# Splitting the last group's left operands where they are made, and keeping three attention tasks under way

## The chip, the cores and the metric

The kernel runs on one core of a Trainium2 chip. A core has five engines that run side by side and meet at semaphores: TensorE (PE, the matmuls), VectorE (DVE), ScalarE (ACT), GpSimd (POOL) and SyncE (SP, which here only starts DMAs). Each takes its instructions in order, so an instruction that waits holds up everything behind it on its engine. The metric is the device time of one launch in microseconds (us). Three runs of the kernel before gave 1162.16, 1162.51 and 1163.85 us: a median of 1162.51.

## The reference, cut to what matters

Two sequences of 512 tokens (b = 0 and 1), model width D = 1024, go through one layer.

```python
h = rms_norm(x, norm1_g) * (1 + sc1) + sh1          # sc, sh, g from silu(c) @ w_ada + b_ada
q_a, k_a, v_a, q_r, k_r, v_r, g_r = split(h @ w_in)
o_a = windowed_attention(q_a, k_a, v_a, sink)       # 8 heads, 2 key groups, |t-s| <= 128, ALiBi
o_r = bidirectional_retention(q_r, k_r, v_r, g_r)   # 4 heads, two decays, group norm, swish gate
x = x + g1 * (concat(o_a, o_r) @ w_out)
h = rms_norm(x, norm2_g) * (1 + sc2) + sh2
x = x + g2 * (square(relu(h @ w_mlp1)) @ w_mlp2)    # 1024 -> 4096 -> 1024
y = rms_norm(x, final_g)
```

## The kernel before, in words

**Precision.** Every large product is made of three: each float32 operand is split into a high part (a cast to a reduced float32, fp32r, on ACT) and a low part (operand minus high part, a subtraction on DVE), and PE adds high x high, high x low and low x high. `split_to` (L840 to L842) is that pair: an ACT cast (L841) and a DVE subtraction (L842).

**The front, up to about 400 us.** Projections of both sequences are a list of units on PE (`run_units`). Beside them a queue of *stages* runs: eight `attn_block`s a sequence (one of four query blocks for one of two key groups) and four `ret_head`s a sequence. Each is a generator; `tick_stage` keeps two of them under way and lets one take a step between two pieces of projection. A `yield 2` asks for a pause of two such pieces before the next step, so that ACT, DVE and POOL finish before PE needs the result. Two of these pauses stand ahead of transposes on PE: `ppt` (L417, attention's probabilities) and `pyb` (L490, retention's normalised output). `norm_x1` prepares sequence 1 (x tiles, `x_rstd`, `x_scale`, then eight transposed columns) and is begun by a hook behind unit 9. The stages take PSUM from five `aux` banks.

**MLP 1, from about 500 to 829 us.** Products of 2x2 blocks are made in seven instead of eight products (Winograd's form of Strassen's algorithm), named P1, P2, P6, P7, P5, P4, P3. A `FirstPair` n (0 to 15) makes two rows of 128 hidden columns; its seven products are 12 matmuls each. Between them `prep` splits the next pair's weights. At its end `store` (L960) combines the squared-ReLU results into the seven *left operands* of MLP 2, each 128x512 float32 (256 KB), and writes them to DRAM through SP's queue (L970): `spill[g][p, :, i, :]`, with g = n // 4 the group and i = n % 4 the place in it. The results lie in tiles `u` (the squared blocks) and `s` (their sums).

**MLP 2, from about 829 us to the end.** Four groups g of seven products of 48 matmuls. `load_u(g, p)` brings back a left operand in two halves h of 512 KB (tiles `ur`, L1275), two steps ahead; `prep(g, p)` (L1278 on) splits it (tiles `uc`, high and low) and the weight block (tiles `wc`), one step ahead. So each `prep` issues four ACT casts and four DVE subtractions of 128x1024. `gather` adds the banks into four accumulators on DVE. The first pair of steps of MLP 2 is prepared within pair 15.

**The last group** runs P1, P2, P6, P7, P4, P5, P3. Here the result is also gated, added to the residual rows `x2r` (`final_rows` loads them behind P2), normalised and stored: `gated_sums` (L1349, L1350) for accumulators that are complete but for one product, `gated_bank` (L1356, L1357) for a bank straight from PE, `squares` (L1362 on ACT, L1365 on POOL), `finish` (L1369 on POOL, L1373 on DVE, then the output DMA). Quadrant (0,0) is gated behind P6 and (0,1) behind P7, with the squares of (0,0).

**What sets the order.** A scheduler places the instructions on each engine from the written order and its own costs; DMAs wrapped in `in_order` keep the written one. Buffers: 32 tiles `r4` and 4 tiles `lx` of 512 KB, 8 tiles `f2` of 256 KB. POOL starts few DMAs: two decay tables, the sink and eight rows of gates (L155, L156, L158, L292).

Of the kernel before, what the change touches and what calls it, by code (L numbers as in the profile page):

```python
# [30 lines left out]
def trunk_kernel(ctx, tc, x0, x1, c0, c1, w_ada, b_ada, norm1_g, w_in, attn_sink, decay_f, decay_b,  # L31
# [352 lines left out]
    def attn_block(b, g, i, qs, k_, a, mix):  # L384
# [27 lines left out]
        for hh in range(4):  # L412
            if hh % 2 == 0:
                nc.scalar.activation(st[hh][:, :w], st[hh][:, :w], AF.Copy, scale=rden[:, hh:hh + 1])
            else:
                nc.vector.tensor_scalar(st[hh][:, :w], st[hh][:, :w], rden[:, hh:hh + 1], None, ALU.mult)
        yield 2  # L417
        pts = []
# [21 lines left out]
    def ret_head(b, h, q_, k_, v_, sg, mix):  # L440
# [46 lines left out]
        for t in range(NT):  # L487
            nc.vector.tensor_scalar(yn[:, t * P:(t + 1) * P], pn[:, t * P:(t + 1) * P], mv[:, t, 0:1],
                                    rs[:, t:t + 1], ALU.subtract, ALU.mult)
        yield 2  # L490
        pb = aux_bank(f"pyb_{nm}")
# [84 lines left out]
    def tick_stage(force=False):  # L576

        while stages and len(active) < 2:
            kind, start = stages.pop(0)
            active.append([start(), 0, kind])  # L580
        for a in active:
            if a[1] <= clock[0] or force:
                wait = next(a[0], "end")
                if wait == "end":
                    active.remove(a)
                else:
                    a[1] = clock[0] + wait
                return True
        return False
# [244 lines left out]
    hc = [[None, None] for _ in range(7)]  # L834
    spill = [tc.dram_tile((7, P, GP, 512), F32, name=f"spill{g}") for g in range(NPAIR // GP)]

# [27 lines left out]
    class FirstPair:  # L864
# [95 lines left out]
        def store(self):  # L960
            c11, c12, c21, c22 = self.c
            two = [self.four(f"s_{self.n}_{i}") for i in range(2)]
            s1, s2, s3, s4 = [two[i // 2][:, i % 2, :] for i in range(4)]
            nc.vector.tensor_tensor(s1, c12, c22, ALU.add)
            nc.vector.tensor_sub(s2, s1, c11)
            nc.vector.tensor_sub(s3, c11, c12)
            nc.vector.tensor_sub(s4, c21, s2)
            g, i = divmod(self.n, GP)
            for p, t in ((P1, c11), (P2, c21), (P4, c22), (P5, s1), (P6, s2), (P7, s3), (P3, s4)):
                nc.sync.dma_start(spill[g][p, :, i, :], t)  # L970

# [213 lines left out]
    def norm_x1():  # L1185
        xt = [load_x_tile(1, t) for t in range(NT)]
        for t in range(NT):
            x_scale(xt[t], x_rstd(1, t, xt[t]))
        yield
        yield  # L1190
        for kc in range(KC):
# [5 lines left out]
    for h in range(RH):  # L1197
        units += ret_units(hT[0], 0, h)
    run_units(units, 1.3, {9: lambda: extra.append(norm_x1())}, pace=0.5)
    units = attn_units(hT[1], 1) + ret_v_units(hT[1], 1)  # L1200
# [81 lines left out]
    def prep(g, p):  # L1282
        for h in range(2):
# [8 lines left out]
            src = {P1: b11, P2: b21, P6: b11, P7: b12, P5: t1.get((g, h)), P4: b21, P3: b22}[p]  # L1292
            left[g, p, h] = split_pairs(f"uc_{g}_{p}_{h}", raw_u.pop((g, p, h)))
            right[g, p, h] = split_pairs(f"wc_{g}_{p}_{h}", src)
# [43 lines left out]
    def final_rows(i):  # L1338
        for t in range(4):
            r0 = (t // 2) * S + i * 256 + (t % 2) * P  # L1340
            fin["x", i, t] = r4f(f"x2r_{i}_{t}")
            in_order(nc.sync.dma_start(fin["x", i, t], x2s[r0:r0 + P, :]))
# [71 lines left out]
    for s, (g, p) in enumerate(steps[:-2]):  # L1414
# [14 lines left out]
        if final:  # L1429
            if p == P2:  # L1430
                final_rows(1)
                final_rows(0)
            elif p == P6:
                gated_sums((1, 0))
                gated_sums((0, 0))
            elif p == P7:
                gated_sums((1, 1))
                gated_sums((0, 1))
                for t in range(4):
# [38 lines left out]
```

## Time and profile before

| | value |
|---|---|
| runs, median of three | 1162.51 us (1162.16 to 1163.85) |
| the profiled execution's own time | 1161.89 us |
| its span in the profile | 1160.1 us (1.8 us below its own time) |
| PE busy | 1109.4 us, 96% |
| DVE busy | 933.4 us, 80% |
| ACT busy | 494.0 us, 43% |
| POOL busy | 69.0 us, 6% |
| DMA traffic | 224.37 MB, mean 193 GB/s |

The profile is one execution. An engine's share is an average over stages with different limits, so the views that matter are the ones by stretch of time: windows that give every engine's busy time and the clock granted to PE, the order of instructions in time on one engine, and the list of who waited for whom. In a row of instructions `out<-in` are the names of the program's tiles; in a row of the order in time the two numbers ahead are the start and the time of that row, and a bracket at the end is idle time before it and what ended it. Where such a row stands for several instructions (x2), consecutive ones overlap a little, so starts tell more than durations.

### The profile page before, as it was taken

The numbers are of one execution on the slowest core, as the hardware profiler recorded it, in microseconds if no ns is written. First come the engines' busy times: TensorE is split into PE (matmuls) and PEld (weight loads), VectorE is DVE, ScalarE is ACT, GpSimd is POOL, SyncE is SP. The second block draws the span as 40 slices with busy tenths as digits, with TensorE's granted clock in tenths as the row PEclk, the third lists the DMA queues.
The fourth block names the chain that finished last, engine by engine and source line by source line (L and its number), as shares of the span: only waits on it lengthen the run. The fifth ranks groups of instructions, "written<-read, shape, count | busy, mean of one in ns | idle before, by whom it ended". The sixth has DMA issues, their size and how long they took to land.

```text
span 1160.1 us, 14470 instructions
## 1 busy us (share of the span) xinstructions
PE 1109.4 (96%) x5167; PEld 903.8 (78%) x5167; DVE 933.4 (80%) x1550; ACT 494.0 (43%) x846; POOL 69.0 (6%) x79
## 2 busy tenths in 40 slices
PE   5899999999999999999999999999999999999975
PEld 3578787777888788888788888888778888888854
DVE  5888988978888697689998778866696866968896
ACT  4456765435563234346333333332455333432341
POOL 3620001000000000000000000000000000000012
PEclk9999999999999999999999999999999999999988
DMA  9796677655455489941654455443866364464413
GB/s 289 238 283 211 214 230 272 218 193 190 155 167 199 156 303 333 343 148 46 214 204 155 164 165 189 155 163 103 287 230 237 106 195 137 144 200 139 184 37 145
DMA packets 124112, 224.37 MB, mean 193 GB/s; under 512 B 8500, under 2 KB 59780, under 8 KB 124040
## 3 DMA queue, kind: packets, MB, share of 16 engines
q1 hardware_dynamic: 111144, 217.14, 55.8%
q10 hardware_dynamic: 12544, 6.29, 1.9%
q8 instruction: 40, 0.66, 0.3%
q0 software_dynamic: 352, 0.03, 0.1%
q14 instruction: 32, 0.26, 0.1%
HBM read 152.36 MB, written 71.06 MB: 193 GB/s over the span
## 4 chain that ended last, share of the span: by engine, by line
PE 75%; DVE 11%; DMA 5%; issue 3%; ACT 3%; POOL 2%; SPq 0%; ACTq 0%; DVEq 0%; POOLq 0%
PE px_None L936 12%; PE x L1310 12%; PE py_None L936 9%; PE y L1310 9%; PE po L129 2%; PE po L130 2%; PE po L128 2%; DMA raw_ada_g<-in_w_ada_dram 2%; PE po L429 1%; PE ppt L422 1%; PE psc L396 1%; PE pj_rq L129 1%; PE pj_rq L128 1%; PE pj_rv L128 1%; PE pj_rv L130 1%
## 5 line engine op out<-in xcount | busy, mean ns | idle before, releaser
L841 ACT CAST uc_0h<-ur 128x1024 fp32r<-128x1024 f32 x28 | 29.4, 1050 | 67.9 <-PE x L1310 38.1
L1310 PE MATMUL x<-wc_0l,uc_0h 128*128 128x512 f32 x128 | 50.7, 396 | 5.4 <-DVE wc_0l L842 5.4
L1310 PE MATMUL x<-wc_0h,uc_0h 128*128 128x512 f32 x128 | 50.5, 396 | 3.9 <-DVE acc L1356 3.2
L128 PE MATMUL po<-wh_wo,ms 128*128 128x512 f32 x128 | 50.5, 397 | 1.9 <-ACT ms L761 1.9
L1310 PE MATMUL x<-wc_1h,uc_1h 128*128 128x512 f32 x128 | 50.3, 394 | 1.0 <-ACT wc_1h L841 1.0
L1310 PE MATMUL x<-wc_1l,uc_1h 128*128 128x512 f32 x128 | 50.2, 392 | 0.5 <-DVE wc_1l L842 0.5
L1310 PE MATMUL x<-wc_0h,uc_0l 128*128 128x512 f32 x128 | 50.3, 393 | 0.0
L1310 PE MATMUL x<-wc_1h,uc_1l 128*128 128x512 f32 x128 | 50.1, 391 | 0.0
L129 PE MATMUL po<-wl_wo,ms 128*128 128x512 f32 x128 | 49.8, 391 | 0.3 <-DVE wl_wo L103 0.3
L842 DVE TENSOR_TENSOR uc_0l<-ur,uc_0h 128x1024 fp32r<-128x1024 f32 x28 | 34.2, 1222 | 19.6 <-ACT uc_0h L841 15.9
L130 PE MATMUL po<-wh_wo,ms 128*128 128x512 f32 x128 | 49.6, 390 | 0.0
L255 DVE SCALAR_TENSOR_TENSOR adacc_c<-raw_ada_c,cact,adacc_c 128x512 f32<-128x512 f32 x56 | 39.8, 748 | 6.7 <-DMA raw_ada_c<-in_w_ada_dram 5.7
L841 ACT CAST wc_s4h<-raw_w 128x1024 fp32r<-128x1024 f32 x16 | 16.8, 1053 | 62.8 <-PE px_None L936 46.1
L406 ACT ACTIVATE st<-st,negm 128x256 f32<-128x256 f32 (+1 forms) x64 | 35.2, 556 | 18.8 <-DVE negm L401 18.8
L841 ACT CAST wc_0h<-w 128x1024 fp32r<-128x1024 f32 x24 | 25.2, 1049 | 42.4 <-DVE w L1289 16.3
L255 DVE SCALAR_TENSOR_TENSOR adacc_g<-raw_ada_g,cact,adacc_g 128x512 f32<-128x512 f32 x56 | 40.3, 747 | 2.1 <-DMA raw_ada_g<-in_w_ada_dram 1.8
L842 DVE TENSOR_TENSOR wc_0l<-w,wc_0h 128x1024 fp32r<-128x1024 f32 x24 | 29.3, 1221 | 13.5 <-ACT wc_0h L841 13.4
L936 PE MATMUL py_None<-hch,wc_a 128*128 128x512 f32 x120 | 39.7, 390 | 0.1
L936 PE MATMUL px_None<-hch,wc_a 128*128 128x512 f32 x120 | 39.6, 391 | 0.0
L936 PE MATMUL px_None<-hch,wc_s 128*128 128x512 f32 x120 | 39.4, 389 | 0.0
L1310 PE MATMUL y<-wc_1l,uc_1h 128*128 128x512 f32 x96 | 37.5, 391 | 0.6 <-DVE wc_1l L842 0.6
L1310 PE MATMUL y<-wc_0h,uc_0h 128*128 128x512 f32 x96 | 37.6, 392 | 0.0
(397 smaller groups left out, 3484.8 us busy)
## 6 DMA issues: line engine op xcount, KB each, us to landing
ur<-spill SPq DMA_DIRECT2D x56, 512.0 KB, 4.3
raw_w<-in_w_mlp_dram SPq DMA_DIRECT2D x32, 512.0 KB, 3.8
spill<-s SPq DMA_DIRECT2D x64, 256.0 KB, 3.7
w<-in_w_mlp_dram SPq DMA_DIRECT2D x32, 512.0 KB, 5.4
spill<-u SPq DMA_DIRECT2D x48, 256.0 KB, 2.3
raw_ada_g<-in_w_ada_dram SPq DMA_DIRECT2D x16, 512.0 KB, 4.3
raw_ada_c<-in_w_ada_dram SPq DMA_DIRECT2D x16, 512.0 KB, 4.0
raw_ada<-in_w_ada_dram SPq DMA_DIRECT2D x12, 512.0 KB, 8.8
```

The source lines that it names most:

```text
L128: nc.tensor.matmul(ps, lhs[0], rhs[0], start=start, stop=False)
L129: nc.tensor.matmul(ps, lhs[0], rhs[1], start=False, stop=False)
L130: nc.tensor.matmul(ps, lhs[1], rhs[0], start=False, stop=stop)
L255: nc.vector.scalar_tensor_tensor(acc[b], src, cb, acc[b], ALU.mult, ALU.add)
L396: nc.tensor.matmul(psc[:, :w], qs[hh][:, isl], k_[:, s, j0 * P:j1 * P], start=(s == 0), stop=(s == 1))
L406: nc.scalar.activation(st[hh][:, :w], st[hh][:, :w], AF.Exp, bias=negm[:, hh:hh + 1], scale=0.125, accum_out=den[:, hh:hh + 1])
L422: nc.tensor.transpose(pt[:, hh * P:(hh + 1) * P], st[hh][:, jj * P:(jj + 1) * P], ident)
L429: nc.tensor.matmul(po, va[:, j0 + jj, g].rearrange("p s e -> p (s e)"), pts[jj][:, s, :], start=(jj == 0 and s == 0), stop=(jj == nj - 1 a ...
L841: nc.scalar.copy(hi, src)
L842: nc.vector.tensor_sub(lo, src, f(hi))
L936: self.last = nc.tensor.matmul(bank[:, cs], x[:, k, :], y, start=first and k == 0 and i == 0, stop=last and k == 3 and i == 2, skip_group_ ...
L1310: nc.tensor.matmul(out, u[x][:, i % 2, ts_], w[y][:, i % 2, :], start=first and i == 0 and k == 0, stop=end and i == GP - 1 and k == 2, sk ...
```

## The change

Five parts.

1. **`store` of the last group** (pairs 12 to 15): each of the seven operands is split at once. ACT casts it into a new `f2` tile `uh`, DVE subtracts in place, and two DMAs, of the high and of the low part, are started by GpSimd. `spill` of the last group has room for both parts.
2. **`load_u` of the last group** brings the two parts of a half straight into `r4` tiles `uh` and `ul` on SP's queue (two DMAs of 512 KB a half instead of one), and `prep` splits the weight alone.
3. **The rows of the end**: `x2r` of i = 1 go to `lx` tiles behind P2, those of i = 0 to `r4` tiles behind P6; the gating of (0,0) moves from P6 to P7, that of (0,1) with the squares of (0,0) from P7 to P4.
4. **Stages**: up to three under way, at most two of a kind; the pauses ahead of `ppt` and `pyb` become three.
5. **`norm_x1`** starts behind unit 7, takes a pause before each x tile and three behind them.

```diff
-        yield 2
+        yield 3
         pts = []
...
-        yield 2
+        yield 3
         pb = aux_bank(f"pyb_{nm}")
...
-        while stages and len(active) < 2:
-            kind, start = stages.pop(0)
-            active.append([start(), 0, kind])
+        for s_ in list(stages):
+            if len(active) == 3:
+                break
+            if sum(a[2] == s_[0] for a in active) < 2:
+                stages.remove(s_)
+                active.append([s_[1](), 0, s_[0]])
...
-    spill = [tc.dram_tile((7, P, GP, 512), F32, name=f"spill{g}") for g in range(NPAIR // GP)]
+    NG = NPAIR // GP
+    spill = [tc.dram_tile((7, P, GP, 512), F32, name=f"spill{g}") for g in range(NG - 1)]
+    spill.append(tc.dram_tile((7, P, 2, GP, 512), F32, name=f"spill{NG - 1}"))
...
-                nc.sync.dma_start(spill[g][p, :, i, :], t)
+                if g < NG - 1:
+                    nc.sync.dma_start(spill[g][p, :, i, :], t)
+                else:
+                    hi = f2(f"uh_{self.n}_{p}", F32R)
+                    split_to(hi, t.bitcast(F32R), t)
+                    nc.gpsimd.dma_start(spill[g][p, :, 0, i, :], f(hi))
+                    nc.gpsimd.dma_start(spill[g][p, :, 1, i, :], t)
...
         for t in range(NT):
+            yield
             x_scale(xt[t], x_rstd(1, t, xt[t]))
-        yield
-        yield
+        for _ in range(3):
+            yield
...
-    run_units(units, 1.3, {9: lambda: extra.append(norm_x1())}, pace=0.5)
+    run_units(units, 1.3, {7: lambda: extra.append(norm_x1())}, pace=0.5)
...
         for h in range(2):
+            if g == ng - 1:
+                left[g, p, h] = r4(f"uh_{g}_{p}_{h}"), r4(f"ul_{g}_{p}_{h}")
+                for s in range(2):
+                    in_order(nc.sync.dma_start(f(left[g, p, h][s]), spill[g][p][:, s, 2 * h:2 * h + 2, :]))
+                continue
...
-            left[g, p, h] = split_pairs(f"uc_{g}_{p}_{h}", raw_u.pop((g, p, h)))
+            if (g, p, h) in raw_u:
+                left[g, p, h] = split_pairs(f"uc_{g}_{p}_{h}", raw_u.pop((g, p, h)))
...
-            fin["x", i, t] = r4f(f"x2r_{i}_{t}")
+            fin["x", i, t] = (lx if i else lambda n: r4(n, F32))(f"x2r_{i}_{t}").rearrange("p a n -> p (a n)")
...
                 final_rows(1)
+            elif p == P6:
                 final_rows(0)
-            elif p == P6:
                 gated_sums((1, 0))
-                gated_sums((0, 0))
             elif p == P7:
                 gated_sums((1, 1))
+                gated_sums((0, 0))
+            elif p == P4:
                 gated_sums((0, 1))
```

**DVE in the last group, from the gathering of P7's first half to the weights of P4 and P5.** In the rows, `uc` and `wc` are left and right operands (5 is P4 and 4 is P5, by the place in the list of products), `acc` the accumulators, `x2r` the rows of the residual; the text behind the arrow is what is read. Before:

```order
L842 TENSOR_TENSOR uc_5_0l<-ur_5_0_9519,uc_5_0h 128x1024
L1324 TENSOR_TENSOR acc_0_8036<-y_3_0_9627,acc_0_8036 128x1024
L842 TENSOR_TENSOR wc_5_0l<-w_3_10_0_9191,wc_5_0h 128x1024
L842 TENSOR_TENSOR uc_5_1l<-ur_5_1_9521,uc_5_1h 128x1024
L842 TENSOR_TENSOR wc_5_1l<-w_3_10_1_9193,wc_5_1h 128x1024
L1324 TENSOR_TENSOR acc_1_8063<-y_3_1_9653,acc_1_8063 128x1024
L1349 TENSOR_TENSOR acc_0_8036<-acc_0_8036,fgate_1_9349 128x512 x2
```

The same place of the changed kernel:

```order
L1342 TENSOR_TENSOR acc_0_8148<-y_3_0_9715,acc_0_8148 128x1024
L1368 TENSOR_TENSOR x2r_1_9683<-x2r_1_9683,acc_0_7922 128x512
L1367 TENSOR_TENSOR acc_0_8148<-acc_0_8148,fgate_1_9465 128x512 x2
L1368 TENSOR_TENSOR x2r_0_9607<-x2r_0_9607,acc_0_8148 128x512
L1368 TENSOR_TENSOR x2r_1_9609<-x2r_1_9609,acc_0_8148 128x512
L1368 TENSOR_TENSOR x2r_2_9685<-x2r_2_9685,acc_1_7949 128x512
L847 TENSOR_TENSOR wc_5_0l<-w_3_10_0_9307,wc_5_0h 128x1024
L847 TENSOR_TENSOR wc_5_1l<-w_3_10_1_9309,wc_5_1h 128x1024
L1342 TENSOR_TENSOR acc_1_8175<-y_3_1_9741,acc_1_8175 128x1024
```

The `uc` rows are gone, and additions to the rows of i = 0 (`x2r_1`, `x2r_2` with `acc_0_7922` and `acc_1_7949`, quadrant (0,0)) have come in from an earlier place.

**DVE at the seam of pair 15 and group 0**: from the sums of `store` on. Before:

```order
L964 TENSOR_TENSOR s_0_7764<-u_0_7608,u_1_7609 128x512
L966 TENSOR_TENSOR s_1_7765<-u_0_7608 128x512
L965 TENSOR_TENSOR s_0_7764<-s_0_7764,u_0_7608 128x512
L967 TENSOR_TENSOR s_1_7765<-u_1_7609,s_0_7764 128x512
L842 TENSOR_TENSOR uc_1_0l<-ur_1_0_7680,uc_1_0h 128x1024
L842 TENSOR_TENSOR wc_1_0l<-w_0_10_0_7676,wc_1_0h 128x1024
L842 TENSOR_TENSOR uc_1_1l<-ur_1_1_7682,uc_1_1h 128x1024
L842 TENSOR_TENSOR wc_1_1l<-w_0_10_1_7678,wc_1_1h 128x1024
```

In the changed kernel, from the last of the four sums on:

```order
L972 TENSOR_TENSOR s_1_7849<-u_1_7693,s_0_7848 128x512
L847 TENSOR_TENSOR uc_1_0l<-ur_1_0_7764,uc_1_0h 128x1024
L847 TENSOR_TENSOR u_0_7692<-u_0_7692,uh_0_7854 128x512
L847 TENSOR_TENSOR wc_1_0l<-w_0_10_0_7760,wc_1_0h 128x1024
L847 TENSOR_TENSOR u_1_7693<-u_1_7693,uh_1_7859 128x512
L847 TENSOR_TENSOR uc_1_1l<-ur_1_1_7766,uc_1_1h 128x1024
L847 TENSOR_TENSOR s_0_7848<-s_0_7848,uh_4_7869 128x512
L847 TENSOR_TENSOR wc_1_1l<-w_0_10_1_7762,wc_1_1h 128x1024
L847 TENSOR_TENSOR s_0_7848<-s_0_7848,uh_2_7874 128x512
L847 TENSOR_TENSOR s_1_7849<-s_1_7849,uh_3_7879 128x512
L847 TENSOR_TENSOR s_1_7849<-s_1_7849,uh_6_7884 128x512
```

The subtractions of the new splits are dealt out among those that prepare P2 of group 0 (`uc_1`, `wc_1`); three come behind them.

**GpSimd's queue, pair 15.** Before, the last rows of gates are followed by the squares of the end:

```order
L292 DMA gates<-adacc_g_0_1_5706 16x1x32
L292 DMA gates<-adacc_g_1_0_6587 16x1x32
L292 DMA gates<-adacc_g_1_1_6588 16x1x32
L1365 TENSOR_SCALAR msf_0_0_9698<-ssf_0_0_9695 128x1
L1365 TENSOR_SCALAR msf_1_0_9703<-ssf_1_0_9700 128x1
```

In the changed kernel 56 DMAs stand there, 14 for each pair; pair 15's are:

```order
L980 DMA spill_120<-uh_0_7854 128x512
L980 DMA spill_120<-uh_1_7859 128x512
L980 DMA spill_120<-uh_5_7864 128x512
L980 DMA spill_120<-uh_4_7869 128x512
L981 DMA spill_120<-u_1_7693 128x512
L980 DMA spill_120<-uh_2_7874 128x512
L980 DMA spill_120<-uh_3_7879 128x512
L981 DMA spill_120<-u_0_7692 128x512
L980 DMA spill_120<-uh_6_7884 128x512
L981 DMA spill_120<-u_1_7693 128x512
L981 DMA spill_120<-s_0_7848 128x512 x2
L981 DMA spill_120<-s_1_7849 128x512 x2
```

High parts (`uh`) and low parts (`u` and `s`, in place) leave on one queue; the tile `u_0`, whose `lx` buffer the operand of P6 in group 0 takes next, leaves in the eighth.

## The prediction

> **What bounds the kernel now.** The page comes first. PE is busy for 96% of the span, so 51 us of idle time are all there is to win, and only where they lie.
>
> ```profile
> PE 1109.4 (96%) x5167; PEld 903.8 (78%) x5167; DVE 933.4 (80%) x1550; ACT 494.0 (43%) x846; POOL 69.0 (6%) x79
> L841 ACT CAST uc_0h<-ur 128x1024 fp32r<-128x1024 f32 x28 | 29.4, 1050 | 67.9 <-PE x L1310 38.1
> L842 DVE TENSOR_TENSOR uc_0l<-ur,uc_0h 128x1024 fp32r<-128x1024 f32 x28 | 34.2, 1222 | 19.6 <-ACT uc_0h L841 15.9
> ```
>
> The last two rows are one half of the splits of left operands in MLP 2 (the other half has names uc_1). The second view is the windows of the last group: columns are the length, then busy time and count of PE, PEld, DVE, ACT and POOL, then the clock granted to PE, the DMA share and GB/s.
>
> ```profile
> 1100.00:1105.00 5.00, 5.00 (x23) 3.81 (x21) 5.00 (x6) 5.00 (x9) 1.00 (x2) 1.00 0.36 105
> 1105.00:1110.00 5.00, 4.39 (x20) 3.38 (x19) 5.00 (x8) 3.62 (x4) 0.00 (x0) 1.00 0.31 108
> 1110.00:1115.00 5.00, 0.47 (x3) 0.04 (x1) 5.00 (x8) 0.00 (x0) 0.00 (x0) 0.92 0.00 0
> 1115.00:1120.00 5.00, 4.12 (x10) 3.25 (x11) 5.00 (x7) 0.00 (x0) 0.00 (x0) 0.50 0.00 0
> ```
>
> DVE is busy for all of these 20 us, while PE does almost nothing for 5 and then runs 10 matmuls in 4.12 us at a granted clock of 0.50. DVE is the bound here. The third view, the order in time, says why (PE rows, two of them from the start of P2 in group 0, then DVE rows).
>
> ```profile
> 838.73 0.39 PE L1310 MATMUL x<-wc_1h,uc_1h 128*128 128x512 f32 x1
> ...
> 840.09 0.39 PE L1310 MATMUL y<-wc_0h,uc_0h 128*128 128x512 f32 x1
> ...
> 1097.67 0.39 PE L1310 MATMUL y<-wc_1h,uc_1l 128*128 128x512 f32 x1
> 1109.85 0.61 PE L1310 MATMUL x<-wc_0h,uc_0h 128*128 128x512 f32 x2
> 1115.88 0.79 PE L1310 MATMUL x<-wc_0l,uc_0h 128*128 128x512 f32 x1 [5.42 <-DVE wc_0l L842]
> ...
> 1100.04 1.23 DVE L842 TENSOR_TENSOR uc_0l<-ur,uc_0h 128x1024 fp32r<-128x1024 f32 x1
> 1101.18 1.23 DVE L1324 TENSOR_TENSOR acc<-y,acc 128x1024 f32<-128x1024 f32 x1
> ...
> 1103.44 1.23 DVE L842 TENSOR_TENSOR uc_1l<-ur,uc_1h 128x1024 fp32r<-128x1024 f32 x1
> 1104.58 1.23 DVE L842 TENSOR_TENSOR wc_1l<-w,wc_1h 128x1024 fp32r<-128x1024 f32 x1
> ...
> 1106.85 1.30 DVE L1349 TENSOR_TENSOR acc<-acc,fgate 128x512 f32<-128x512 f32 x2
> 1108.05 1.30 DVE L1350 TENSOR_TENSOR x2r<-x2r,acc 128x512 f32<-128x512 f32 x2
> ...
> 1113.46 1.23 DVE L842 TENSOR_TENSOR uc_0l<-ur,uc_0h 128x1024 fp32r<-128x1024 f32 x1
> ...
> 1115.73 1.23 DVE L842 TENSOR_TENSOR uc_1l<-ur,uc_1h 128x1024 fp32r<-128x1024 f32 x1
> ...
> 1120.40 1.23 DVE L842 TENSOR_TENSOR uc_0l<-ur,uc_0h 128x1024 fp32r<-128x1024 f32 x1
> ...
> 1123.61 0.69 DVE L1356 TENSOR_TENSOR acc<-y,fgate 128x512 f32<-128x512 f32 x1 [0.68 <-PE y L1310]
> 1124.22 1.22 DVE L842 TENSOR_TENSOR uc_1l<-ur,uc_1h 128x1024 fp32r<-128x1024 f32 x1
> ...
> 1126.33 0.69 DVE L1356 TENSOR_TENSOR acc<-y,fgate 128x512 f32<-128x512 f32 x1 [0.29 <-PE y L1310]
> 1126.94 1.22 DVE L842 TENSOR_TENSOR wc_1l<-w,wc_1h 128x1024 fp32r<-128x1024 f32 x1
> ...
> 1128.67 1.28 DVE L1356 TENSOR_TENSOR acc<-x,fgate 128x512 f32<-128x512 f32 x2
> ...
> 1155.44 1.42 DVE L1373 SCALAR_TENSOR_TENSOR x2r<-x2r,rf,fgain 128x512 f32<-128x512 f32 x2 [1.87 <-POOL rf L1369]
> ```
>
> The first two rows are six matmuls apart: 0.2267 us each where nothing waits, so a step of 48 takes 10.88 us and a pair's 84 take 19.04. From starts, a 128x1024 subtraction takes 1.135 us back to back (1103.44 to 1104.58) and a 128x512 operation 0.60 (1106.85 to 1108.05 for two). PE finishes the tiles that the gathering of P7 needs at 1098.06 (1097.67 + 0.39), and DVE starts it at 1101.18, 3.1 us late. From 1128.67, the first bank of P5, to the end of the span (1160.1) lie 31.4 us, in which DVE waits in turn for banks and for the normalising factor from POOL, as in the last row. That stretch the change leaves as it is.
>
> **The last group: -7.6 us.** All 14 `uc` subtractions and 14 casts of the group go. What lies on the path is DVE's queue from P7's gathering to 1128.67. Before, it holds 13 instructions of 128x1024 and 19 of 128x512: 14.8 + 11.5 = 26.2 us, plus 0.97 of waiting for PE (0.68 + 0.29) and 0.3 of small gaps, the 27.5 between the two starts. Five of the 13 are `uc` rows (1103.44, 1113.46, 1115.73, 1120.40, 1124.22); one (1126.94, P3's second weight) stands in the changed order behind the first bank of P5. Four additions of quadrant (0,0) come in from earlier. So the changed queue holds 7 long and 23 short: 7.9 + 13.9 = 21.8 us, and it can start at 1098.1, since the `uc` rows that made it late (the last at 1100.04) are gone: 1119.9. I count no wait for PE in it: P7 ends 24 matmuls behind 1098.06, at 1103.5; P4 begins with its second weight, about 1104, and its last bank, with five matmuls of P5 ahead of it, is due at 1104 + 53 x 0.2267 = 1116.0, where DVE is ready for it at 1116.3. The banks of P5's first two tiles come at about 1117.6 and 1120.3. Then the 1.1 us of the displaced subtraction and the same 31.4: 1119.9 + 1.1 + 31.4 = 1152.4, against 1160.1. Bounds: -3.3 if only the five `uc` rows count, less the four additions (5.7 - 2.4); -11.6 if DVE is never late and the stretch starts with P5's first bank at 1117.1. What is late next is the tail itself: DVE in order, ACT's squares, POOL's two small steps.
>
> The operands now come as 28 loads of 512 KB in place of 14. They are free to start when their `r4` buffers are, two steps of 10.88 us ahead, and the DMA share in the windows above is 0.00 to 0.36; I count nothing.
>
> **The new splits: +1.0 us.** Each of the four pairs gets 7 casts and 7 subtractions of 128x512, so 7 x 0.605 = 4.2 us of DVE. The windows below hold the `store` of pairs 12 and 14 (first two rows; pair 13's reads like 12's) and of pair 15 with the start of MLP 2 (last two).
>
> ```profile
> 767.00:786.20 19.20, 19.20 (x86) 15.68 (x85) 13.39 (x20) 6.48 (x10) 0.48 (x1) 1.00 0.43 144
> ...
> 805.40:824.60 19.20, 19.20 (x87) 15.89 (x85) 9.06 (x13) 5.03 (x7) 0.00 (x0) 1.00 0.69 223
> 824.60:843.90 19.30, 18.61 (x82) 15.13 (x81) 15.75 (x18) 9.53 (x11) 0.00 (x0) 1.00 0.88 299
> 843.90:863.10 19.20, 17.64 (x77) 13.96 (x77) 18.75 (x18) 10.56 (x11) 0.00 (x0) 1.00 0.58 203
> ```
>
> Pairs 12 to 14 have DVE at 13.4 and 9.1 of 19.2 us: 17.6 and 13.3 fit, and ACT (6.5 plus at most 7 x 1.05) too. Their cover is this free time on DVE. Pair 15 falls where DVE is busy for 34.5 of 38.5 us; 4.2 more do not fit into 4.0 without moving something. Against that, SP's queue no longer holds pair 15's spills ahead of the weights of P6, for which DVE waited:
>
> ```profile
> 841.67 1.23 DVE L1287 TENSOR_TENSOR t<-w,w 128x1024 f32<-128x1024 f32 x1 [2.48 <-DMA w<-in_w_mlp_dram]
> ```
>
> I expect most to be made up there. Bounds: +4.2 if all of it reaches PE, -2.2 if instead PE's idle time in the two windows (0.69 + 1.56) vanishes. I take +1.0, nearer the middle.
>
> **GpSimd's queue: 0.** 56 DMAs of 256 KB that the trace does not show on this queue. The nearest rows are its small ones (2 KB of gates, and a table for 128 partitions), and how the former and the loads of left operands land:
>
> ```profile
> 772.41 0.48 POOL L292 DMA_DIRECT2D gates<-adacc_g  x1 [95.20 <-ACT adacc_g L291]
> 772.35 0.68 DVE L958 TENSOR_TENSOR u<-u 128x512 f32<-128x512 f32 x1
> 1.28 0.76 POOL L155 DMA_DIRECT2D dec<-in_ret_decay_fwd_dram  x1 [0.35 <-issue]
> gates<-adacc_g POOLq DMA_DIRECT2D x2, 2.0 KB, 2.5
> ur<-spill SPq DMA_DIRECT2D x56, 512.0 KB, 4.3
> ```
>
> At 0.48 to 0.76 us each a pair's 14 take 6.7 to 10.6 of 19.0 us, and POOL does nothing else there: covered. The other end is 2.5 us each, the landing time, if the engine were held that long: 35 us a pair, which is the first rival. I take the value of the table, 0.76, since it too is written for 128 partitions. [...]
>
> **Three tasks and `norm_x1`: -1.0 us.** Of 100 to 400 us the list of PE's waits has five rows, 3.0 us in all; first and last:
>
> ```profile
> PE pj_rk L130 <- DVE wl_rk L103: 0.8, 1, 0.8
> ...
> PE px L312 <- DVE x L321: 0.4, 1, 0.4
> ```
>
> The others are 0.7 (`mix`), 0.6 (`pyb` behind `ryn`) and 0.5 (`px` behind `rv_x`). The longer pauses and the third task can remove the waits of the stages, the changed `norm_x1` those of `px`; the weights' 0.8 stays. Bounds: -3.0, and +5.6 as in the third rival. I take -1.0.
>
> **Sum.** 1160.1 - 7.6 + 1.0 + 0 - 1.0 = 1152.5 us of span. The median of the runs stands 2.4 above the profiled span (its own time was 1161.89), so 1152.5 + 2.4 = **1154.9 us**.
>
> **The rivals.**
> 1. *GpSimd's queue falls behind; slower.* The queue keeps up while a DMA takes less than 19.04 / 14 = 1.36 us. Above, each pair starts later than its data is ready. The first operand of P6 in group 0 takes the `lx` buffer of `u_0`, the eighth DMA of pair 15; P6 is due 10.88 behind P2, at 851. Pair 12's sums begin here:
>
> ```profile
> 773.07 0.69 DVE L964 TENSOR_TENSOR s<-u,u 128x512 f32<-128x512 f32 x1
> ```
>
>    At 1.9 us a DMA (between 1.36 and 2.5) pair 12 starts at 773, pair 15 at 773 + 3 x 26.6 = 853, the eighth is through at 868, and landing 2.5, load 4.3 (the page's median for `ur`) and split 2.2 (an ACT cast and a subtraction) make 877: 26 us late, **1181**; at 2.5 us it would be 1211. Against it: the rows of 0.48 and 0.76. For it: their size is a hundredth of the new ones.
> 2. *No room at the seam.* Pair 15's 4.2 us of DVE reach PE whole: 3.2 more, **1158.1**. For it: DVE at 18.75 of 19.2. Against it: the 2.48 of waiting.
> 3. *Banks in front.* Two retention heads hold an `aux` bank each for their sums, which leaves three of five for scores and transposes; if each of eight heads costs PE one wait of the size of `mix` (0.7), 5.6 us come instead of -1.0: **1161.5**, no change. For it: DVE is at 80% there. Against it: every wait is short today.
> 4. *A larger gain*: the tail shortens too and the seam gains: **1150.5**.
>
> That the change does not do what it says would need loads of `uh` and `ul` that come late; with a DMA share of 0.36 at most I fold that into the second rival.
>
> **How the numbers follow.** Forecast 0.62, first rival 0.11, second 0.10, third 0.09, fourth 0.08. Two tenths of a per cent, 2.3 us, is about what a measurement of this kernel can tell from no change. Faster: 0.62 + 0.10 + 0.08 = 0.80; within: 0.09; slower: 0.11. The range 1150 to 1162 holds all but the first rival and some edges.
>
> **What would show it.** Right: no `uc` rows in the last group, PE without the idle of 5.42 us and without a granted clock of 0.50 at P5, the first bank of P5 taken near 1120 and 31 to 33 us from there to the end. GpSimd's DMAs under 1.36 us each, pair 15's done before 850. PE's waits in front under 3 us. Wrong: POOL busy without a break from 773 past 850, PE idle at P6 of group 0, or new waits of `psc`, `ppt` or `py` for banks. The forecast falls if DVE's queue in the last group fills with other waits, so that P5's first bank stays at 1128.

## The result, and the profile after

The changed kernel takes 1164.01 us (median of 22 runs) against 1162.34 us for the kernel before (22 runs of the same jobs): a ratio of 1.0016 [1.0009, 1.0023]. The change costs a little where 7.6 us were forecast to go, and the time lies above the range. The profiled execution took 1164.17 us, with a span of 1162.4.

In the changed kernel line numbers stand higher: the cast of `split_to` is L846, its subtraction L847, the matmul of MLP 2 L1328, the gathering L1342, `gated_sums` L1367 and L1368, `gated_bank` L1374 and L1375, `finish` L1387 and L1391. The page first: the rows of PE, of GpSimd's queue (q0; packets, MB, share of 16 engines) and of all DMA traffic.

```profile
PE 1110.2 (96%) x5167; PEld 906.4 (78%) x5167; DVE 932.4 (80%) x1564; ACT 495.4 (43%) x860; POOL 97.0 (8%) x135
q0 software_dynamic: 4832, 14.71, 3.5%
DMA packets 126577, 239.06 MB, mean 206 GB/s; under 512 B 9172, under 2 KB 60452, under 8 KB 126504
```

Nothing in the totals shows where the time went. A table by stage does: the start of each stage's first matmul in the order in time of PE.

| stage | begins before | begins after | its length, after minus before |
|---|---|---|---|
| front (to the first matmul of MLP 1) | 0 | 0 | +2.1 |
| MLP 1 | 504.80 | 506.89 | +1.7 |
| P1 and P2 of group 0 | 829.07 | 832.87 | +0.1 |
| P6 of group 0 | 850.97 | 854.88 | +4.1 |
| P7 of group 0 up to P7 of the last group | 863.98 | 872.03 | 0.0 |
| from P7 of the last group to the end | 1092.46 | 1100.53 | -5.8 |
| end of the span | 1160.1 | 1162.4 | sum +2.3 |

The last group did gain, and the front and P6 of group 0 gave back more than that. Of the +1.7 in MLP 1, 1.2 lie in its first 71 us, which have a stretch of low granted clock (the column before the last two of the windows) in this one execution:

```profile
520.00:540.00 20.00, 17.35 (x111) 15.57 (x110) 17.84 (x34) 12.02 (x22) 1.10 (x2) 0.91 0.04 16
```

In e1, e2 and e9 below, with the same code there, these 71 us have their old length. So about 0.5 of the 1.7 belongs to the change in this profile; e1 and e9 have 1.0 and 1.1 us more in MLP 1.

**The last group.** The windows of the stretch that the prediction showed (length; busy time and count of PE, PEld, DVE, ACT, POOL; granted clock, DMA share, GB/s):

```profile
1100.00:1105.00 5.00, 5.00 (x24) 4.14 (x23) 5.00 (x9) 1.48 (x2) 0.00 (x0) 1.00 0.97 371
1105.00:1110.00 5.00, 5.00 (x23) 4.14 (x23) 5.00 (x9) 0.00 (x0) 0.00 (x0) 1.00 0.61 247
1110.00:1115.00 5.00, 4.60 (x20) 3.49 (x20) 5.00 (x7) 3.05 (x3) 0.00 (x0) 1.00 0.60 210
1115.00:1120.00 5.00, 5.00 (x22) 3.88 (x22) 5.00 (x8) 0.00 (x0) 0.00 (x0) 1.00 0.02 5
```

PE has no gap of 5 us any more and its full clock, while DVE is as full as before. The order in time on DVE:

```profile
1106.17 1.23 DVE L1342 TENSOR_TENSOR acc<-y,acc 128x1024 f32<-128x1024 f32 x1
...
1110.92 1.22 DVE L847 TENSOR_TENSOR wc_0l<-w,wc_0h 128x1024 fp32r<-128x1024 f32 x1
...
1128.13 0.69 DVE L1374 TENSOR_TENSOR acc<-x,fgate 128x512 f32<-128x512 f32 x1
...
1156.08 1.42 DVE L1391 SCALAR_TENSOR_TENSOR x2r<-x2r,rf,fgain 128x512 f32<-128x512 f32 x2 [1.87 <-POOL rf L1387]
```

P7 begins 8.1 us later than before, so times are counted from it: the first bank of P5 (1128.13) is taken 27.6 us behind P7's start, against 36.2 before.

**The front and the seam.** PE's list of waits (us in total, times, longest) has two rows near its head that the kernel before does not have in this size:

```profile
PE pj_rv L128 <- DVE ks L347: 5.1, 1, 5.1
PE x L1328 <- ACT wc_1h L846: 3.1, 1, 3.1
```

The first lies at 90.97 us, in the front; the second at 861.95, in P6 of group 0. The next two parts follow each to its source.

At 90.97 PE waits for `ks` of a second attention block. ACT's order in time in the changed kernel shows what `ks` stood behind, a weight of the gate's modulation (`adacc_g`, from the background list) that was still on its way:

```profile
81.23 1.05 ACT L97 CAST wh_rv<-raw_rv 128x1024 fp32r<-128x1024 f32 x1
87.47 0.72 ACT L253 ACTIVATE adacc_g<-raw_ada_g,cact 128x512 f32<-128x512 f32 x1 [5.19 <-DMA raw_ada_g<-in_w_ada_dram]
88.22 0.58 ACT L344 CAST ks<-first 64x512 fp32r<-64x512 f32 x1
```

and in the kernel before:

```profile
81.03 1.05 ACT L97 CAST wh_rv<-raw_rv 128x1024 fp32r<-128x1024 f32 x1
82.11 0.58 ACT L344 CAST ks<-first 64x512 fp32r<-64x512 f32 x1
```

There `ks` follows `wh_rv` at once; now it comes 6 us later. The longer pause ahead of `ppt` leaves room for a step of the background list in between (e6, with the short pauses, has no such wait), and in order on ACT `ks` stood behind that step's wait of 5.19 us (it starts 0.03 us behind the step's end). The windows around it:

```profile
88.00:90.00 2.00, 0.00 (x0) 0.00 (x0) 1.33 (x2) 1.94 (x5) 0.00 (x0) 1.00 1.01 392
90.00:92.00 2.00, 1.03 (x3) 0.87 (x4) 1.96 (x4) 1.98 (x5) 0.00 (x0) 0.63 0.28 100
92.00:94.00 2.00, 2.00 (x7) 1.61 (x6) 1.52 (x4) 1.95 (x4) 0.00 (x0) 0.52 0.00 0
```

The wait costs twice: PE stands for 5.12 us, and then works at a granted clock of 0.63 and 0.52 in the two windows behind it.

At the seam, the rows of the changed kernel's order in time (POOL, SP, ACT, DVE, DVE, ACT, PE) make a chain:

```profile
838.71 0.54 POOL L981 DMA_DIRECT2D spill<-u  x1 [0.48 <-DVE u L847]
...
845.37 4.71 SPq L1292 DMA_DIRECT2D ur<-spill  x3
...
852.83 1.05 ACT L846 CAST uc_0h<-ur 128x1024 fp32r<-128x1024 f32 x1 [7.71 <-DMA ur<-spill]
...
853.91 1.23 DVE L847 TENSOR_TENSOR uc_0l<-ur,uc_0h 128x1024 fp32r<-128x1024 f32 x1 [2.01 <-ACT uc_0h L846]
...
859.60 1.22 DVE L1306 TENSOR_TENSOR w<-w,t 128x1024 f32<-128x1024 f32 x1
...
860.85 1.04 ACT L846 CAST wc_1h<-w 128x1024 fp32r<-128x1024 f32 x1 [5.07 <-DVE w L1306]
...
861.95 1.22 PE L1328 MATMUL x<-wc_1h,uc_1h 128*128 128x512 f32 x2 [3.05 <-ACT wc_1h L846]
```

The tile `u_0`, whose buffer the operand of P6 takes, is the eighth DMA of pair 15 and leaves GpSimd at 838.71. The load into that buffer is issued at 845.37, 6.7 us on, and its cast runs at 852.83, another 7.5 on. DVE, in order, stands behind that operand and makes the second weight of P6 (`w`, L1306) late. Before, `u_0` was not split and left long ahead of MLP 2 (at 817.62), and the cast of this operand ran at 841.25:

```profile
841.25 1.05 ACT L841 CAST uc_0h<-ur 128x1024 fp32r<-128x1024 f32 x1
```

From the start of MLP 2 that is 12.2 us, against 20.0 now. What the two transfers met is in the windows, before and then after (the last two columns are the DMA share and GB/s):

```profile
830.00:840.00 10.00, 10.00 (x46) 8.28 (x45) 8.13 (x10) 3.81 (x4) 0.00 (x0) 1.00 0.85 245
840.00:850.00 10.00, 10.00 (x46) 8.29 (x45) 7.88 (x7) 3.96 (x4) 0.00 (x0) 1.00 0.98 382
```

```profile
820.00:830.00 10.00, 10.00 (x45) 8.09 (x44) 9.17 (x12) 5.49 (x7) 4.39 (x9) 1.00 1.01 379
830.00:840.00 10.00, 8.98 (x40) 7.12 (x39) 8.71 (x13) 6.94 (x11) 4.30 (x8) 1.00 1.03 411
840.00:850.00 10.00, 10.00 (x45) 8.28 (x45) 8.84 (x11) 2.69 (x3) 2.70 (x5) 1.00 1.04 401
```

The DMA engines are full for 30 us (shares of 1.01 to 1.04): pair 15 now writes twice the bytes (high and low parts) just when the loads of weights and operands for MLP 2 run. Before, the share was 0.88 from 820 to 830 and 0.85 and 0.98 behind it. That the bytes make the transfers slow is put to the test in e8. GpSimd's own queue is not the cause; its engine is busy for 4.39 of 10 us at most in these windows.

### The profile page after: what moved, and what is told of

Same layout as the page of the kernel before. It is cut to its first block, busy times and chain, and to the rows that moved or that the text cites. A ratio compares the mean times of both kernels' runs of the same rounds, so it can differ in the third digit from the quotient of the medians.

```text
span 1162.4 us, 14622 instructions
## 1 busy us (share of the span) xinstructions
PE 1110.2 (96%) x5167; PEld 906.4 (78%) x5167; DVE 932.4 (80%) x1564; ACT 495.4 (43%) x860; POOL 97.0 (8%) x135
## 5 line engine op out<-in xcount | busy, mean ns | idle before, releaser
L846 ACT CAST wc_0h<-w 128x1024 fp32r<-128x1024 f32 x24 | 25.1, 1048 | 71.5 <-PE x L1328 28.2
L846 ACT CAST uc_0h<-ur 128x1024 fp32r<-128x1024 f32 x21 | 22.1, 1051 | 60.9 <-PE x L1328 22.2
L847 DVE TENSOR_TENSOR wc_0l<-w,wc_0h 128x1024 fp32r<-128x1024 f32 x24 | 29.3, 1221 | 18.5 <-ACT wc_0h L846 18.5
L1328 PE MATMUL x<-wc_1h,uc_1h 128*128 128x512 f32 x96 | 38.0, 398 | 3.1 <-ACT wc_1h L846 3.1
L846 ACT CAST wc_s4h<-raw_w 128x1024 fp32r<-128x1024 f32 x16 | 16.8, 1052 | 52.7 <-PE px_None L941 32.1
L1328 PE MATMUL x<-wc_0h,uc_0h 128*128 128x512 f32 x96 | 37.4, 392 | 1.0 <-ACT u L962 1.0
L1328 PE MATMUL x<-wc_0l,uc_0h 128*128 128x512 f32 x96 | 37.5, 390 | 0.7 <-DVE wc_0l L847 0.7
L1328 PE MATMUL x<-wc_1l,uc_1h 128*128 128x512 f32 x96 | 38.0, 396 | 0.0
L454 ACT CAST rsc<-rsf 128x512 fp32r<-128x512 f32 x32 | 19.8, 617 | 42.7 <-DVE rsf L452 42.5
L1328 PE MATMUL x<-wc_1h,uc_1l 128*128 128x512 f32 x96 | 37.7, 393 | 0.0
L1328 PE MATMUL x<-wc_0h,uc_0l 128*128 128x512 f32 x96 | 37.4, 389 | 0.0
L847 DVE TENSOR_TENSOR uc_0l<-ur,uc_0h 128x1024 fp32r<-128x1024 f32 x21 | 25.6, 1221 | 14.5 <-ACT uc_0h L846 14.5
L846 ACT CAST wc_1h<-w 128x1024 fp32r<-128x1024 f32 x24 | 25.1, 1048 | 24.9 <-DVE w L1306 23.1
```

Source lines behind the costliest of these rows:

```text
L454: nc.scalar.copy(sc[sb][:, 0, :], sf)
L846: nc.scalar.copy(hi, src)
L847: nc.vector.tensor_sub(lo, src, f(hi))
L1328: nc.tensor.matmul(out, u[x][:, i % 2, ts_], w[y][:, i % 2, :], start=first and i == 0 and k == 0, stop=end and i == GP - 1 and k == 2, sk ...
```

## The experiments

Theory at the start: the loss has two places, the wait for `ks` in the front and P6's wait at the seam, where the operand waits for the store of `u_0`. The rivals: the front is innocent, GpSimd's queue is slow, DVE and ACT have no room at the seam. That the DMA engines are full came in with e5 and e8; the loss behind the last DVE instruction was in none of the theories. Each kernel was timed against the kernel before (1162.08, 1162.05 and 1161.63 us in the three jobs).

### e1: the change without its front

```diff
-        yield 3
+        yield 2
...
-        for s_ in list(stages):
...
+        while stages and len(active) < 2:
...
-    run_units(units, 1.3, {7: lambda: extra.append(norm_x1())}, pace=0.5)
+    run_units(units, 1.3, {9: lambda: extra.append(norm_x1())}, pace=0.5)
```

Both pauses go back to two, and `norm_x1` loses its new pauses as well.

> The change without its front (two tasks, pauses of 2, the old norm_x1); only the last group's operands and the order of its end are new. Theory: in the profile of the changed kernel the loss has two places, +3.3 us ahead of MLP 1 (one wait of 5.1 us at 85 us) and +4.6 us at the seam of MLP 1 and MLP 2, against -5.8 us from P7 of the last group to the end. So this kernel loses the +3.3: 1162.3 + 4.6 - 5.8 = about 1161.1 us (1160 to 1162), without the 5.1 us wait at 85 us. Rival (the front is innocent, the wait at 85 us is chance): as the whole change, 1164.

Measured: 1161.11 us (11 runs), ratio 0.9991 [0.9981, 1.0]. The wait of 5.1 is gone and MLP 1 begins at 505.45. P6 of group 0 takes 16.65 us (13.0 before): the loss at the seam belongs to the new splits and their stores, not to the front.

### e2: the front of the change alone

The same hunks the other way round, on the kernel before.

> The kernel before with the front of the change alone (three tasks, pauses of 3, norm_x1). Theory: +3.3 us, about 1165.6 (1164 to 1167), with PE waiting some 5 us at 85 us for the second ks. Rival (front innocent): 1162.3 or, as the prediction had it, 1161.3.

Measured: 1164.18 us (12 runs), 1.0024 [1.0014, 1.0034], with a wait of 5.38 us at 91.42. The front alone loses 2 us and the rest alone gains 1; their sum, +1.1, is near the +1.7 of the whole change.

### e3: the operand of P6 in other buffers

```diff
-(r4 if g == 0 and p in (P1, P2) else lx)
+(r4 if g == 0 and p in (P1, P2, P6) else lx)
```

> As e1_back_only, and the two loads of P6's left operand in group 0 go to r4 buffers in place of lx, so that they no longer wait for the low part of pair 15 on GpSimd's queue. Theory (the seam's loss is that wait): the +4.6 falls to +1 or less, 1156.5 to 1158. Rival (DVE and ACT have no room for pair 15's splits): as e1_back_only, 1161.

Measured: 1168.4 us (6 runs), 1.0056 [1.0043, 1.0068]. A miss. The operand no longer waits for `u_0`, but another load of an operand stands ahead of it in SP's order and waits for a store of a `u` tile. Behind that load the four loads of weights are issued from 838.74 on (from 826.90 on in e1), and the two loads of P6's operand only from 841.43 on. The row of the loads of weights, and SP's list of waits (us, times, longest):

```profile
838.74 2.60 SPq L1278 DMA_DIRECT2D w<-in_w_mlp_dram  x4
```

```profile
SPq L1288 <- DMA spill<-u: 17.3, 3, 12.7
```

So it doesn't tell the two theories apart: with other buffers the wait for a store moves to another load, and SP's order hands it on.

### e4: all stores on SP's queue

```diff
-                    nc.gpsimd.dma_start(spill[g][p, :, 0, i, :], f(hi))
-                    nc.gpsimd.dma_start(spill[g][p, :, 1, i, :], t)
+                    nc.sync.dma_start(spill[g][p, :, 0, i, :], f(hi))
+                    nc.sync.dma_start(spill[g][p, :, 1, i, :], t)
```

> The whole change with the 56 store DMAs on SP's queue in place of GpSimd's. Theory (what is late is the operand of P6 behind the store's low parts, not GpSimd): the loads stand behind the same stores in SP's order, so no gain, 1164 to 1168. Rival (GpSimd's queue itself is slow): the seam's loss shrinks, 1160.

Measured: 1171.09 us (5 runs), 1.0085 [1.0071, 1.0099]: no gain, as expected, but 3 us above the expected range. In SP's order the loads stand behind the stores; PE waits 2.67 and 0.83 us at P1 and 2.42, 1.56 and 0.99 at P6. About 2 us of the loss lie in the front, where the code is that of the changed kernel (MLP 1 begins at 509.03, against 506.89). Of the two queues GpSimd's is the better one for these stores (1164.01 us for the changed kernel against 1171.09).

### e5: pair 15 stored whole

On e1. Pair 15's quarter of each operand is stored whole, and split in the last group; the load of the high part, cut short in a hunk not shown, leaves that quarter out.

```diff
+                elif i == GP - 1:
+                    nc.sync.dma_start(spill[g][p, :, 1, i, :], t)
...
+            elif h == 1:
+                uh, ul = left[g, p, h]
+                split_to(uh[:, 1, :], ul[:, 1, :], f(ul[:, 1, :]))
```

> As e1_back_only, but pair 15 stores its operands whole, on SP's queue, and a quarter of each operand of the last group is split there as before (7 casts and 7 subtractions of 128x512 return). Theory (the seam's loss comes from pair 15's stores, which double the bytes and hold the buffers of P6's operand in a stretch where the DMA engines are full): the seam's loss falls from 4.6 to about 1, the gain at the end from 5.8 to some 3.5: 1159.5 (1158.5 to 1161). Rival (pairs 12 to 14 on GpSimd's queue are enough to delay group 0): 1162 to 1164.

Measured: 1160.4 us (12 runs), 0.9986 [0.9976, 0.9997], as expected. P6 takes 13.1 us, with the waits of before; part of the gain in the last group goes back, since its quarter of the splits returns to DVE, and PE waits 1.98 and 2.05 us there.

### e6: three tasks and `norm_x1`, with the short pauses

The two hunks of e2 other than the pauses, on the kernel before.

> The kernel before with three tasks and the new norm_x1, but pauses of 2. Theory (the longer pause ahead of the attention transposes puts the gate's activation, which waits for its weights, ahead of the second ks on ACT): no wait of 5 us at 85 us, 1160 to 1162. Rival (three tasks do it): 1164 as e2_front_only.

Measured: 1166.94 us (4 runs), 1.0044 [1.0027, 1.006]. The wait for `ks` is gone, as the theory had it, but the time is a miss: a third task with the new `norm_x1`, without the longer pauses, costs 5 us. PE's order in time has a wait that no list held before,

```profile
193.35 0.79 PE L128 MATMUL py<-rsc,rv 128*128 128x512 f32 x1 [4.07 <-ACT rsc L454]
```

and a granted clock of 0.50 in the windows from 192 to 198. Ahead of `rsc`, DVE holds a step of `adacc_g` from the background list, which waits 0.63 us for its DMA, and a weight's split, which waits 1.45 us for ACT. That these two make it late is read from the order, not tried.

### e7: the front alone, its background list begun one unit later

On e2.

```diff
-    background.extend([ada_gate(0), ada_columns(1, True), ada_columns(1, False)])
...
-    run_units(units, 1.3, {7: lambda: extra.append(norm_x1())}, pace=0.5)
+    run_units(units, 1.3, {7: lambda: extra.append(norm_x1()), 1: lambda: background.extend([ada_gate(0), ada_columns(1, True), ada_columns(1, False)])}, pace=0.5)
```

> As e2_front_only, with the background work of the gates begun one unit later, so that its activation stands behind both ks on ACT. Theory (the front's loss is that one wait, and three tasks and longer pauses gain behind it): 1164.2 - 5.4 - 1.3 of half clock = 1157.5 to 1159.5. Rival (what e2 won back behind the wait was only slack): 1162.

Measured: 1156.8 us (8 runs), 0.9959 [0.9943, 0.9975], a little better than expected and 7.4 us better than e2. ACT's order in time:

```profile
83.08 0.58 ACT L344 CAST ks<-first 64x512 fp32r<-64x512 f32 x1
```

`ks` is back behind `wh_rv`. Where the background list begins decided the sign of the whole front: +2.1 us as in the change, -5.3 one unit later.

### e8: half the high parts not stored

On e1.

```diff
-                    nc.gpsimd.dma_start(spill[g][p, :, 0, i, :], f(hi))
+                    if i < 2:
+                        nc.gpsimd.dma_start(spill[g][p, :, 0, i, :], f(hi))
...
-                    in_order(nc.sync.dma_start(f(left[g, p, h][s]), spill[g][p][:, s, 2 * h:2 * h + 2, :]))
+                    in_order(nc.sync.dma_start(f(left[g, p, h][s]), spill[g][p][:, s, 2 * h * s:2 * h * s + 2, :]))
```

> As e1_back_only, with the 14 stores of the high parts of pairs 14 and 15 left out (the loads of the last group's second half take the high parts of pairs 12 and 13 in their place), 3.7 MB less to write at the seam; DVE, ACT, and the wait of P6's operand for the low parts are as they were. Theory A (full DMA engines): P6 of group 0 starts without its 3 us wait, 1156 to 1158. Theory B (the chain low part, its store, buffer, load): the wait stays, 1160 to 1161.

Measured: 1156.44 us (4 runs), 0.9953 [0.9937, 0.9969]. All casts and subtractions are still there, and only 14 transfers are gone, so that the last group gets wrong high parts for pairs 14 and 15. The store of `u_0`, the load into its buffer and the cast (POOL, SP, ACT):

```profile
835.54 0.54 POOL L979 DMA_DIRECT2D spill<-u  x1 [1.80 <-DVE u L844]
...
838.28 1.77 SPq L1289 DMA_DIRECT2D ur<-spill  x2
...
842.77 1.06 ACT L843 CAST uc_0h<-ur 128x1024 fp32r<-128x1024 f32 x1 [0.82 <-DMA ur<-spill]
```

The store leaves 5.84 us behind the start of MLP 2 (829.70), just as in the changed kernel, but the load is issued 2.7 us behind it in place of 6.7, and its cast follows after 4.5 in place of 7.5. The windows:

```profile
840.00:850.00 10.00, 10.00 (x45) 8.28 (x45) 8.79 (x10) 4.07 (x4) 1.62 (x3) 1.00 0.79 257
```

DVE is as busy as in the changed kernel (8.84) and the DMA share is 0.79 in place of 1.04. So it is the bytes that make the operand late. They are not the whole of P6's loss: PE's waits fall from 3.06 and 0.53 us in e1 to 2.18, and P6 takes 15.18 us, between the 16.65 of e1 and the 13.0 before. The second weight of P6, counted from the start of MLP 2 to its last subtraction (`w`, in e8 at L1303), starts at 24.6 us, against 25.6 in e1 and 23.5 before and in e5. That the time fell into the theory's range is in part luck: of the 3.6 us by which the span is shorter than that of e1, 1.0 lie ahead of MLP 2, 1.5 in P6 and 1.1 behind DVE's last instruction (more on that in the last section).

### e9 and e10: both remedies on the whole change

e9 is the whole change with the edit of e7; e10 adds that of e5.

> The whole change with the background work of the gates begun one unit later. If the two halves add: 1156.8 (e7) - 1.0 (e1 against before) = 1155.8 (1154.5 to 1157). Rival (they disturb each other): 1158 or more.

> As e9_full_bg1 with pair 15 stored whole as in e5_p15_whole: 1156.8 - 1.7 = 1155.1 (1154 to 1156.5).

Measured: 1155.4 us (5 runs), 0.9946 [0.9934, 0.9958], and 1154.97 us (5 runs), 0.9938 [0.9924, 0.9951]. The halves add up: the front's -5.3 and the rest's -1.0. That e9 comes out near the forecast of 1154.9 is chance: neither half has the size that was forecast for it. In e10 the DMA share is as high for 30 us (1.02, 1.04 and 1.04 from 810 to 840) and P6 still takes 13.1 us. So a high share alone does not make P6 late: pair 15's stores wait for no split there, and the load into `u_0`'s buffer is issued 9.1 us behind the start of MLP 2, against 12.6 in e9.

### e11: pair 15's high parts leave behind P6

On e9. The seven high parts of pair 15 stay in their tiles until the last matmul of P6 in group 0; the low parts, whose buffers are waited for, leave as before. `fin["last"]` is that matmul.

```diff
+                    if i == GP - 1:
+                        held.append((spill[g][p, :, 0, i, :], f(hi)))
+                    else:
+                        nc.gpsimd.dma_start(spill[g][p, :, 0, i, :], f(hi))
...
+        if (g, p) == (0, P6):
+            for d_, t_ in held:
+                x_ = in_order(nc.gpsimd.dma_start(d_, t_))
+                tc.add_manual_dep(x_.ins, fin["last"].ins.name, mybir.DependencyInfo(
+                    mybir.DependencyClass.Sync, mybir.DependencyReason.DATA), reason="late")
```

> As e9_full_bg1, but the seven high parts of pair 15 leave only behind P6 of group 0 (they wait in their f2 buffers), so 1.8 MB less is written at the seam; nothing is left out. Theory (full DMA engines at the seam): P6's wait goes or halves, 1152.5 to 1154. Rival (the chain of the low parts): as e9_full_bg1.

Measured: 1153.6 us (5 runs), 0.9926 [0.9914, 0.9939]: the lowest median of all kernels here, though its interval overlaps those of e9 and e10; nothing of the computation is left out. The windows and then the rows of ACT and PE:

```profile
830.00:840.00 10.00, 10.00 (x46) 8.29 (x45) 9.97 (x13) 4.96 (x6) 3.24 (x6) 1.00 0.84 280
840.00:850.00 10.00, 10.00 (x45) 8.28 (x45) 8.82 (x8) 2.95 (x3) 0.00 (x0) 1.00 0.79 270
```

```profile
841.35 1.05 ACT L847 CAST uc_0h<-ur 128x1024 fp32r<-128x1024 f32 x1 [3.48 <-DMA ur<-spill]
...
852.59 0.73 PE L1331 MATMUL x<-wc_1h,uc_1h 128*128 128x512 f32 x2 [2.18 <-ACT wc_1h L847]
```

Counted from the start of MLP 2 (825.62), the operand is cast after 15.7 us, against 19.1 in e9 and 12.2 before, and the last subtraction for P6's second weight starts at 24.6 us, against 25.8 in e9. P6 takes 14.17 us against 17.6 in e9. Only 0.3 of these 3.4 us is listed waiting; the rest goes with the granted clock, which stays whole here (1.00) and reads 0.50 from 853 to 859 in e9. What is left, 2.18 and 0.53 us of waiting, is 1.1 more than the 1.11 and 0.53 of e5 and e10, which write as many bytes of pair 15 there but have none of its splits on DVE. As in e8 against e5 (24.6 and 23.5), these splits make the weight 1.1 us later.

### e12: the longer pauses with two tasks, background list later

On the kernel before, the pauses and the edit of e7.

> The kernel before with the longer pauses alone, the background begun one unit later: two tasks, old norm_x1. Theory (the longer pauses are what gains in e7): 1157 to 1159. Rival (the third task gains): 1161.5 to 1163.

Measured: 1168.87 us (5 runs), 1.0063 [1.005, 1.0075]. Both expectations missed. In PE's order in time:

```profile
410.33 0.80 PE L128 MATMUL po<-wh_wo,ms 128*128 128x512 f32 x1 [6.04 <-ACT ms L761]
```

This is the output projection, which waits for the last stages; another wait, of 2.64 us for `rsc`, lies at 258.18. It looks as if longer pauses with only two tasks make the stages end late. So the pauses without the third task lose 7 us, the third task without the pauses loses 5 (e6), and together, as e7, they gain 5.3. The pairs are not clean: e6 has the background list at its old place, and e6 with the later list was not run. How much of the gain comes from the pairing stays open.

## Why the prediction was wrong

**The last group, -7.6: measured -5.8.** The step on DVE's queue was right: 27.6 us from P7's start to P5's first bank, 27.4 predicted. From there to the end of DVE's last instruction it took 29.4 us (1156.08 + 1.42 - 1128.13), and the prediction's 1.1 added to the old 28.2 makes 29.3. What failed is that the stretch was called unchanged up to the end of the span (31 to 33 us from P5's first bank; it took 34.3): between DVE's last instruction and the end lie 4.9 us (1162.4 - 1157.5) where there were 3.2 (1160.1 - 1156.86). These 1.7 us are almost the whole error of the term. They are the closing wait of GpSimd's queue, shown in the last section.

**The new splits, +1.0: measured +4.7** (4.1 in P6, 0.6 ahead of it; in e1, 3.6 and 1.0). The step asked whether DVE has room for 4.2 us of subtractions and made it a matter of PE waiting for DVE. DVE's part has about the predicted size: with pair 15's splits the second weight of P6 is made 1.1 us later (e8 against e5, e11 against e10). Two more terms were put at nothing. The transfers make that weight another 1.0 to 1.2 us later (e1 against e8, e9 against e11). The row with a DMA share of 0.88 was quoted in that very place, and yet the new transfers were costed by GpSimd's time to start them, and the rival's by landing times of 2.5 and 4.3 us from the whole page; at the seam a store and the load behind it took 6.7 and 7.5. And a granted clock of 0.73 and 0.50 (861 to 865) follows the wait of 3.05 us: P6's 17.15 us, less 48 matmuls (10.88) and 3.76 us of listed waits, leave 2.5, against 0.6 before. The prediction had shown such a clock in the last group but did not charge it to a new wait. In the changed kernel's profile the weight is made 3.3 us later than before, so about 1 us of that stays without a cause.

**GpSimd's queue, 0: right for the stores, wrong for the end.** That the queue falls behind was the first rival's condition, and it did not: the group of the high parts on the engine's list by lines (busy us, mean ns | idle before) reads

```profile
L980 POOL DMA_DIRECT2D spill<-uh x28 | 15.2, 543 | 124.2 <-ACT uh L846 122.7 <-DMA spill<-uh 0.7 <-ACT wc_0h L846 0.5
```

0.54 us each (0.58 at most in all 56), below the 0.76 assumed and far below the 1.36 from which the queue would fall behind. The one at 838.71 above lies wholly beside a subtraction on DVE,

```profile
838.38 1.23 DVE L847 TENSOR_TENSOR wc_0l<-w,wc_0h 128x1024 fp32r<-128x1024 f32 x1
```

and took 0.54 like the rest; before, the 2 KB of gates at 772.41 took 0.48 wholly beside the DVE row at 772.35. What the term left out is the end of the program, where the queue costs the 1.7 us above.

**Three tasks and `norm_x1`, -1.0: measured +2.1.** Two errors that point in opposite directions. The step read PE's waits of before, asked which would vanish, and did not ask what a longer pause lets in ahead: the gate's step on ACT ahead of `ks`, and its wait for a weight. The order on ACT shows that exchange without any time. And the bound of -3.0, all waits of that list, was no bound: with the background list one unit later the front gains 5.3 to 5.7 (e7; e9 against e1). From 80 us to MLP 1, which begins 5.8 us earlier in e7, PE's idle time falls from 6.15 to 2.90 us and its busy time from 418.65 to 416.12, with the same matmuls; 1.8 of these 2.5 us lie in 128x128 transposes (48.0 to 46.2 in the list by lines). Time that PE loses within and between instructions stands in no list of waits. Why the transposes are shorter was not settled, and the later background list was not tried alone on the kernel before.

**The rivals.** The second (no room at the seam) had the right place, but DVE's part is 1.1 of its 3.2 us; the transfers and the granted clock make the rest. The third (banks in front) gave +5.6; a third task does cost about that when it comes without the pauses (e6), but the wait that the trace shows there is on DVE's and ACT's order, not on a bank.

## What to carry to other kernels

When a change moves work to an emptier engine by way of memory, look at the window where the bytes travel: which buffer each new store holds, which load waits for it, and how full the DMA engines are (the share of 0.88 from 820 to 830 became 1.01 with the new transfers). Charge a new wait of PE with the granted clock behind it too (2.5 us in P6 here, against 0.6 before). When a pause is lengthened, look in the order of every in-order engine for what slips in ahead, and whether that has its data. And of two edits that each lose alone, the pair may win: try halves, but also try the pair with its one bad step mended.

## What the hardware showed that was not expected

**The end of the span grows with DMAs started by GpSimd.** From the end of DVE's last instruction to the end of the span the traces show 3.2 to 3.3 us in the kernels that store without GpSimd (before, e2, e4, e6, e7, e12), 3.75 to 3.8 in those with 42 such DMAs (e5, e8, e10), and 4.85 to 4.9 in those with 56 (the change, e1, e3, e9, e11). No arithmetic stands in this stretch, but the closing instructions of the engines' queues do. Of the program's last line, GpSimd's rows before and after read (count, then shortest, median and longest in ns, first and last start in us):

```profile
L1474 POOLq DRAIN  x3: 40/93/1587, 1154.8 to 1159.9; - x3
L1493 POOLq DRAIN  x3: 40/93/6156, 1155.5 to 1162.1; - x3
```

The longest of the three is the first. It takes 1.59 us in the kernels with 11 DMAs on GpSimd, 5.01 with 42 more and 6.16 with 56 more: 0.08 us for each. Before, it is over at 1156.4, while SP waits for the output DMAs until 1159.3; in the changed kernel SP is through at 1159.9 and this `DRAIN` ends at 1161.6, last of all. That is the 1.7 us. e4 makes the same 56 transfers from SP's queue and its `DRAIN` takes 1.59 and its stretch 3.2 us, so it goes with the queue and not with the transfers. What GpSimd does in that time the traces don't show.

**Behind a wait of 2 to 3 us the granted clock can be 0.50 for as long as the wait lasted, or longer.** Behind the wait of 3.05 us the windows of the changed kernel read

```profile
861.00:863.00 2.00, 1.05 (x2) 0.50 (x2) 2.00 (x2) 2.00 (x3) 0.00 (x0) 0.73 0.13 51
863.00:865.00 2.00, 1.96 (x5) 1.49 (x5) 2.00 (x3) 2.00 (x3) 0.00 (x0) 0.50 0.00 0
```

and the same place of e11, behind 2.18 us,

```profile
853.00:855.00 2.00, 1.47 (x7) 0.97 (x6) 2.00 (x3) 2.00 (x3) 0.00 (x0) 1.00 0.01 2
```

where the clock stays whole; in e8 a wait of the same 2.18 us was followed by 0.50 (857 to 859), and in e9 one of the same 3.05 us by 0.50 from 853 to 859. So a wait of 2.18 us can be enough, as e8 shows, and need not be, as e11 shows. What decides between the two, no run here shows.
